# Closing weight sums made by accumulating transfers, inner sums in four slots and later, the decay of two heads later

## The chip, the cores and the metric

The kernel runs on one core of a Trainium2 chip. The metric is device time in microseconds (us). The engines are PE (TensorE: matrix products), DVE (VectorE), ACT (ScalarE), POOL (GpSimd, here mostly an issuer of transfers) and SP (SyncE, which issues most loads). A wait on an engine holds everything queued behind it on that engine.

## The reference

One layer, T = 1024 rows, width 1024, all in float32:

```
h = rms_norm(x, norm_w) * (1 + scale) + shift        # scale, shift, gate = silu(c) @ ada_w + ada_b
hq, hf, hi, hz, gq, gk, gv, gz, ga, mg = split(h @ w_in)
y_h = hgrn2(hq, hf, hi, hz)     # 8 heads, gated linear attention, decay f = lb + (1 - lb) sigmoid(hf)
y_g = gla(gq, gk, gv, gz, ga)   # 4 heads, decay alpha = sigmoid(ga @ alpha_w + alpha_b) ** (1/16)
merged = sigmoid(mg0) * (y_h @ w_branch[0]) + sigmoid(mg1) * (y_g @ w_branch[1])
out = rms_norm(x + gate * (merged @ w_out), final_norm_w)
```

Both attentions run over chunks of 64 rows with a state of 128 keys per head.

## The kernel before, in words

**Number format.** A float32 operand is split in two parts of a shorter format, hi and lo. One product takes three matmuls (hi·hi, hi·lo, lo·hi). L211 (ACT, a cast) makes hi, L212 (DVE, a subtraction) makes lo; L202 and L203 do the same in other places.

**Seven products instead of eight.** Larger products are done as 2x2 blocks by a scheme with seven products in the order 1, 2, 5, 3, 6, 7, 4. Products 5, 6, 3 and 7 (`SUMS`) use sums of weight blocks. These sums are made ahead of time and kept in DRAM: `v_sums` makes them for the inner stages (DRAM tiles `vs`), `prepare` for the closing stages (DRAM tiles `ws`).

**Memory.** 46 slots of SBUF of 4 KB in each partition are lent out by a pool `S`. A slot that was sent to DRAM (`sent=True`) comes free four units later.

**Stages.** A unit is six matmuls of 128x512 of a main product. The main work runs in this order: q and k of the GLA branch; the GLA values (`Vstage`, units 0 to 56); features of GLA (56 to 104); the HGRN values (second `Vstage`, 104 to 160); features of HGRN (`Fstage`, 160 to 216); the remaining features (L607, 216 to 376); the closing stages `last_stages` in four quarters b = 0 to 3 (L1422, 376 to 600); the output product. L2002 is the matmul of the three inner stages. L1860, L1862, L1884 and L1888 take finished sums from PSUM.

**Side work.** `Stream.weave` is called after each unit and advances three tracks, each a queue of generators: `side` (attention heads), `more` and `back`. An entry `[generator, wait, pace, from]` starts at the unit `from`; a generator yields how many units it wants to rest. Heads 0 to 3 are GLA heads, beginning at about units 49, 88, 127 and 166; eight HGRN heads follow every 24 units from 210. A head loads q (and k) on SP (L1054), prepares decayed copies on DVE and ACT (L657 to L771), has its scores on PE (L665 to L767), brings them to SBUF on ACT (L776, L779, L792, L795), and runs the states (L815, L821) and the outputs (L834, L836). L1019 and L1024 close its output.

**The side work that the change touches.**
- `alpha_side((2, 3))`: decay of heads 2 and 3. Four matmuls L389, then ACT L943, DVE L949 and L950, ACT L953 and L956 (Exp, Ln), DVE L957, ACT L960 (Exp). [...]
- `v_sums(s)`: per half four blocks are loaded by SP (L1829), DVE makes four sums (L1832 to L1838, 128x1024 each), POOL stores them (L1840).
- `prepare`: 16 blocks, each two loads of 512 KB by SP (L1258), four additions 128x512 on DVE (L1266 to L1272) and four stores of 256 KB by POOL (L1274). A flag pauses it between the start of the second inner stage and the thirteenth product of the third.
- `gate_side`: loads and a sum for the output gate.

**What sets the order.** The program is written in the order that `weave` gives; a scheduler then orders each engine's queue. Instructions under `held` keep their program order. `Stream.ahead` loads and splits the operands of the next products when enough slots are free.

Of the kernel before, what the change touches and what calls it, by code (L numbers as in the profile page):

```python
# [10 lines left out]
F32 = mybir.dt.float32  # L11
# [3 lines left out]
ALU = mybir.AluOpType  # L15

P = 128
D = 1024
T = 1024
# [13 lines left out]
SUMS = {5: 0, 6: 1, 3: 2, 7: 3}  # L33
# [56 lines left out]
def hybrid_trunk_kernel(  # L90
# [6 lines left out]
    nc = tc.nc  # L97
    x2, o2 = x[0], out[0]
# [4 lines left out]
    dp = ctx.enter_context(tc.tile_pool(name="dram", bufs=1, space=bass.MemoryType.DRAM))  # L103
# [3 lines left out]
    S = Slots(sp, N_SLOTS)  # L107
# [790 lines left out]
    stream = Stream()  # L898
# [353 lines left out]
    paused = [False]  # L1252

    def load_blocks(b, i):
        src = sources[b][i]
        x = [S.get([4, 2, P]) for _ in range(2)]
        for kh in range(2):
            nc.sync.dma_start(x[kh].rearrange("p k a f -> p k (a f)"),  # L1258
                              src[kh * 512:(kh + 1) * 512, :].rearrange("(k p) f -> p k f", p=P))
        return x  # L1260

    def weight_sums(b, i, x1, x2):
        s1, s2 = S.get([2, 4, P]), S.get([2, 4, P])
        parts = {5: s1[:, 0], 6: s1[:, 1], 3: s2[:, 0], 7: s2[:, 1]}
        add = nc.vector.tensor_add
        held(add(parts[7], x1[:, :, 0], x1[:, :, 1]))  # L1266
        yield 1
        held(add(parts[5], x1[:, :, 1], x2[:, :, 1]))
        yield 1
        held(add(parts[6], parts[7], x2[:, :, 1]))  # L1270
        yield 1
        held(add(parts[3], parts[6], x2[:, :, 0]))  # L1272
        for p, q in SUMS.items():
            nc.gpsimd.dma_start(w_sums[b][i // 2][q][:, i % 2 * 512:i % 2 * 512 + 512],  # L1274
                                parts[p].rearrange("p k f -> p (k f)"))
        S.free(x1, x2)
        S.free(s1, s2, sent=True)
        summed_up.add((b, i))

    def prepare():  # L1280
        todo = [(b, i) for b in range(4) for i in range(4)]
        blocks_of = {}
        for n in range(len(todo) + 1):
            while n < len(todo) and (len(S.free_list) < 11 or paused[0]):
                yield 1
            if n < len(todo):
                blocks_of[n] = load_blocks(*todo[n])
            if n:
                yield from weight_sums(*todo[n - 1], *blocks_of.pop(n - 1))
            yield 5  # L1290


    H = {}
# [54 lines left out]
    def load_duo(b, p, j):  # L1348

        t = raw_w[b, p, j] = S.get([2, 512])  # L1350
        if p in SUMS:
            assert {(b, 2 * j), (b, 2 * j + 1)} <= summed_up
            nc.sync.dma_start(t.rearrange("p a f -> p (a f)"), w_sums[b][j][SUMS[p]])
# [465 lines left out]
    def v_sums(s):  # L1819

        add = nc.vector.tensor_add
        for kk in range(2):
            while len(S.free_list) < 9:
                yield 1
            y = {}
            for at_ in ((0, 1), (1, 1), (0, 0), (1, 0)):
                y[at_] = S.get([2, 512])
                for cols, x in w_block(s, *at_, kk):
                    nc.sync.dma_start(y[at_][:, :, cols], x)  # L1829
# [9 lines left out]
            for p, t in ((5, e), (7, y[0, 0]), (6, y[0, 1]), (3, y[1, 0])):  # L1839
                nc.gpsimd.dma_start(vs_d[s][p][kk], t.rearrange("p a f -> p (a f)"))  # L1840
            S.free(y[1, 1])
            S.free(e, y[0, 0], y[0, 1], y[1, 0], sent=True)
            summed_v.add((s, kk))
            yield 2

# [175 lines left out]
    vjobs[0][10].begins = lambda: load_qk(0)  # L2021
    vjobs[0][12].begins = first_head

    def pause(on):
        paused[0] = on

    vjobs[1][0].begins = lambda: pause(True)
    vjobs[2][12].begins = lambda: pause(False)

    def heads_ready(f):  # L2030
        for h in range(2 * f, 2 * f + 2):
# [15 lines left out]
    def front():  # L2047
# [59 lines left out]
```

## Time and profile before

| | us |
|---|---|
| median of three runs (lowest, highest) | 1184.71 (1183.03, 1186.02) |
| the profiled execution | 1183.32 |
| its span | 1181.6 |
| PE busy | 1148.5 |
| DVE busy | 842.1 |
| ACT busy | 648.5 |
| POOL busy | 138.1 |
| mean granted PE clock (1 is full) | 0.994 |

How to read the rows. A timeline row is: start, duration, engine, line, operation, output <- inputs, partitions x elements, count, and in brackets the idle time before it and what released it. A row that ends in "us in total, times, longest" is a wait. In rows by stretch of time (`from:to`), the engines' busy times are followed by the granted PE clock, the share of the 16 DMA engines that was busy, and GB/s. A row of a group of instructions gives busy time and mean ns of one, then idle time before them.

### The profile page before, as it was taken

The page shows a single profiled execution, that of the slowest core. Times are in us where ns is not written, and L with a number is a line of the kernel's source. Part 1 is how long each engine was busy: PE and PEld are TensorE (multiplying, and loading weights), DVE is VectorE, ACT ScalarE, POOL GpSimd, SP SyncE. Part 2 cuts the span into 40 slices and gives each one's busy share as a digit, 9 for nine tenths or more (in the row PEclk, how much of TensorE's full clock was granted, in tenths as well). Part 3 has the DMA queues.
Part 4 walks back from the last instruction along what each step waited for, and adds up shares of the span by engine and source line. Part 5 has one row for each costly group of instructions (what it writes and reads, how often), then busy time and mean ns, then how long its engine had stood idle before and what let it go on. Part 6 is the DMA issues. An engine that isn't in the chain of part 4 may idle for free.

```text
span 1181.6 us, 20555 instructions
## 1 busy us (share of the span) xinstructions
PE 1148.5 (97%) x8089; PEld 942.3 (80%) x8089; DVE 842.1 (71%) x1316; ACT 648.5 (55%) x964; POOL 138.1 (12%) x285
## 2 busy tenths in 40 slices
PE   6999999899999999999999999999999999999997
PEld 5777877688888888788888887878888888888886
DVE  4755669657686636987787688695643866988994
ACT  5675455543664758646455445576643644534654
POOL 5121112010011101222211111001110000000000
PEclk8999999999999999999999999999999999999999
DMA  9847369667476546988865674355798846334523
GB/s 319 279 150 245 143 220 306 204 200 259 143 248 197 186 160 188 293 269 276 255 220 178 222 241 137 100 179 173 258 317 288 284 144 225 119 117 161 181 93 137
DMA packets 155986, 245.56 MB, mean 208 GB/s; under 512 B 10139, under 2 KB 107473, under 8 KB 155890
## 3 DMA queue, kind: packets, MB, share of 16 engines
q1 hardware_dynamic: 134866, 174.10, 46.7%
q0 software_dynamic: 20976, 70.15, 15.6%
q8 instruction: 63, 1.03, 0.3%
q14 instruction: 33, 0.27, 0.1%
q10 hardware_dynamic: 48, 0.01, 0.0%
HBM read 170.29 MB, written 73.92 MB: 207 GB/s over the span
## 4 chain that ended last, share of the span: by engine, by line
PE 62%; issue 22%; DVE 5%; POOL 4%; ACT 4%; DMA 2%; SPq 0%; POOLq 0%; ACTq 0%; DVEq 0%
PE pd L1422 14%; PE pd L2002 12%; PE pd L607 9%; PE sc_ps L1422 6%; PE pm L1422 6%; PE pd L1599 3%; PE sc_ps L1599 2%; PE pm L834 2%; POOL ws L1274 2%; PE pm L836 1%; PE pm L1599 1%; PE pm L815 1%; PE pd L396 1%; DMA b<-in_x_dram 1%; POOL v L1867 1%
## 5 line engine op out<-in xcount | busy, mean ns | idle before, releaser
L607 PE MATMUL pd<-b,b 128*128 128x512 f32 x1248 | 301.6, 396 | 0.0
L607 PEld LDWEIGHTS pd<-b,b 128*128 128x128 f32 x1248 | 230.6, 188 | 48.5
L2002 PE MATMUL pd<-b,b 128*128 128x512 f32 x1008 | 237.8, 393 | 4.2 <-DVE b L1888 2.5
L2002 PEld LDWEIGHTS pd<-b,b 128*128 128x128 f32 x1008 | 187.6, 188 | 45.7 <-ACT b L211 2.9
L1422 PE MATMUL pd<-b,b 128*128 128x512 f32 x720 | 169.4, 390 | 0.0
L1422 PEld LDWEIGHTS pd<-b,b 128*128 128x128 f32 x720 | 134.8, 188 | 28.2
L212 DVE TENSOR_TENSOR b<-b,b 128x1024 fp32r<-128x1024 f32 x92 | 110.9, 1222 | 57.1 <-ACT b L211 52.3
L1365 DVE TENSOR_TENSOR b<-b,b 128x1024 fp32r<-128x1024 f32 x56 | 68.2, 1222 | 57.8 <-ACT b L1364 44.7
L211 ACT CAST b<-b 128x1024 fp32r<-128x1024 f32 x92 | 93.3, 1047 | 11.5 <-PE pd L2002 3.8
L1364 ACT CAST b<-b 128x1024 fp32r<-128x1024 f32 x56 | 58.7, 1051 | 63.3 <-PE pm L1422 17.7
L1422 PE MATMUL sc_ps<-b,b 128*128 128x512 f32 x324 | 77.5, 390 | 0.1
L1342 DVE TENSOR_TENSOR b<-b,b 128x1024 fp32r<-128x1024 f32 x48 | 57.9, 1221 | 23.9 <-ACT b L1341 18.7
L1341 ACT CAST b<-b 128x1024 fp32r<-128x1024 f32 x48 | 49.9, 1051 | 41.5 <-PE pd L1422 16.0
L1422 PE MATMUL pm<-b,b 128*128 128x512 f32 x300 | 71.1, 389 | 0.0
L1422 PEld LDWEIGHTS sc_ps<-b,b 128*128 128x128 f32 x324 | 60.6, 188 | 13.0 <-ACT scT L779 0.5
L1422 PEld LDWEIGHTS pm<-b,b 128*128 128x128 f32 x300 | 56.3, 188 | 11.7
L203 DVE TENSOR_TENSOR b<-b,b 128x1024 fp32r<-128x1024 f32 (+1 forms) x37 | 35.7, 976 | 27.5 <-ACT b L202 27.2
L396 PE MATMUL pd<-b,b 128*128 128x512 f32 x192 | 51.9, 403 | 0.9 <-ACT b L202 0.8
L1274 POOL DMA_DIRECT2D ws<-b x64 | 34.5, 540 | 138.2 <-DVE b L1266 52.8
L834 PE MATMUL pm<-scT,b 128*128 128x128 f32 x256 | 47.5, 278 | 2.8 <-DVE b L821 2.6
L726 DVE TENSOR_TENSOR b<-b,tot 128x512 f32<-128x512 f32 x36 | 24.8, 688 | 30.4 <-PE sc_ps L767 29.2
L834 PEld LDWEIGHTS pm<-scT,b 128*128 128x128 f32 x256 | 38.5, 191 | 7.1 <-DVE b L821 4.8
(333 smaller groups left out, 1749.9 us busy)
## 6 DMA issues: line engine op xcount, KB each, us to landing
b<-in_w_in_dram SPq DMA_DIRECT2D x64, 512.0 KB, 6.0
ws<-b POOLq DMA_DIRECT2D x64, 256.0 KB, 5.4
b<-ws SPq DMA_DIRECT2D x32, 512.0 KB, 4.1
b<-in_w_in_dram SPq DMA_DIRECT2D x52, 256.0 KB, 4.0
b<-fx SPq DMA_DIRECT2D x24, 512.0 KB, 4.7
b<-in_x_dram SPq DMA_DIRECT2D x16, 512.0 KB, 6.1
b<-in_ada_w_dram SPq DMA_DIRECT2D x32, 256.0 KB, 6.4
v<-b POOLq DMA_DIRECT2D x32, 256.0 KB, 4.0
```

The lines of the kernel that those rows point to most:

```text
L211: held(nc.scalar.copy(hi, src))
L212: nc.vector.tensor_sub(lo, src, hi.bitcast(F32))
L396: nc.tensor.matmul(accs[f], wg(a, d, f), b[d][:, half * 512:half * 512 + 512], start=(d == 0 and n == 0), stop=(d == KT - 1 and n == 2))
L607: nc.tensor.matmul(ps[th][0:w, :], a[:, k, 0:w], b[:, th * 512:(th + 1) * 512], start=(k == 0 and n == 0), stop=(k == KT - 1 and n == 2))
L834: nc.tensor.matmul(o, vch(ch)[:, vh * P:(vh + 1) * P], scT[:, ch, :], start=True, stop=(ch == 0))
L1274: nc.gpsimd.dma_start(w_sums[b][i // 2][q][:, i % 2 * 512:i % 2 * 512 + 512], parts[p].rearrange("p k f -> p (k f)"))
L1342: nc.vector.tensor_sub(lo, src, hi.bitcast(F32))
L1364: nc.scalar.copy(hi, t)
L1365: nc.vector.tensor_sub(lo, t, hi.bitcast(F32))
L1422: nc.tensor.matmul(o, a[:, sl], c, start=(p in (1, 5) and kt == 0 and n == 0), stop=(kt == 3 and n == 2), skip_group_check=True)
L1599: nc.tensor.matmul(o, a, b, start=(p in (1, 5) and kt == 0 and n == 0), stop=(kt == 3 and n == 2), skip_group_check=True)
L2002: nc.tensor.matmul(st.bank[i], l_[:, i * P:(i + 1) * P], r_, start=(p in (1, 5) and kk == 0 and a == 0 and n == 0), stop=(kk == 1 and a == ...
```

## The change

Four things are edited.

1. `prepare` makes no sums on DVE any more. For each quarter b it issues 26 transfers on POOL, all from DRAM to DRAM, in the order of a list `CHAIN`: the first block of a sum is copied into `ws`, further blocks are added by the transfer itself (`accum_op=ALU.add`), and two sums start as a copy of another one (1 MB each). A block transfer is 256 KB in rows of 128 floats. There is one unit between two of them and 2.25 more behind each entry of the list. It starts at unit 214, without the pause.
2. `v_sums` adds in place and needs four slots instead of five, in another order of loads and sums; it waits for 8 free slots instead of 9. Both calls start at unit 56, on the track `more`.
3. `alpha_side((2, 3))` goes from `more` (from unit 50) to `back` (from unit 86).
4. `gate_side` starts at unit 300 instead of 320.

```diff
-    w_sums = [[[dp.tile([P, T], F32, name=f"ws{b}{j}{i}") for i in range(4)] for j in range(2)] for b in range(4)]
+    w_sums = [{p: dp.tile([P, 4, 512], F32, name=f"ws{b}{p}") for p in SUMS} for b in range(4)]
...
-    def weight_sums(b, i, x1, x2):
-        s1, s2 = S.get([2, 4, P]), S.get([2, 4, P])
-        parts = {5: s1[:, 0], 6: s1[:, 1], 3: s2[:, 0], 7: s2[:, 1]}
-        add = nc.vector.tensor_add
-        held(add(parts[7], x1[:, :, 0], x1[:, :, 1]))
-        yield 1
-        held(add(parts[5], x1[:, :, 1], x2[:, :, 1]))
-        yield 1
-        held(add(parts[6], parts[7], x2[:, :, 1]))
-        yield 1
-        held(add(parts[3], parts[6], x2[:, :, 0]))
...
+    CHAIN = ((7, (0, 0)), (5, (0, 1)), (7, (0, 1)), (5, (1, 1)), (6, 7), (6, (1, 1)), (3, 6), (3, (1, 0)))
 
     def prepare():
-        todo = [(b, i) for b in range(4) for i in range(4)]
...
+        for b in range(4):
+            def block(kh, a, b=b):
+                src = sources[b]
+                return [src[i][kh * 512:kh * 512 + 512, a * P:a * P + P] for i in range(4)]
+            done = set()
+            for p, src in CHAIN:
+                first = p not in done
+                done.add(p)
+                if isinstance(src, int):
+                    held(nc.gpsimd.dma_start(w_sums[b][p], w_sums[b][src]))
+                else:
+                    for i, x in enumerate(block(*src)):
+                        x = x.rearrange("(k p) f -> p k f", p=P)
+                        y = w_sums[b][p][:, i].rearrange("p (k f) -> p k f", f=P)
+                        if first:
+                            held(nc.gpsimd.dma_start(y, x))
+                        else:
+                            held(nc.gpsimd.dma_start(y, x, accum_op=ALU.add))
+                        yield 1
+                yield 2.25
+            summed_up.add(b)
...
         for kk in range(2):
-            while len(S.free_list) < 9:
+            while len(S.free_list) < 8:
                 yield 1
             y = {}
-            for at_ in ((0, 1), (1, 1), (0, 0), (1, 0)):
+            for at_ in ((0, 1), (0, 0), (1, 1), (1, 0)):
...
-            e = S.get([2, 512])
-            held(add(e, y[0, 1], y[1, 1]))
-            yield 2
             held(add(y[0, 0], y[0, 0], y[0, 1]))
             yield 2
-            held(add(y[0, 1], y[0, 0], y[1, 1]))
+            held(add(y[0, 1], y[0, 1], y[1, 1]))
             yield 2
-            held(nc.vector.scalar_tensor_tensor(y[1, 0], y[0, 1], -1.0, y[1, 0], ALU.mult, ALU.subtract))
...
+            held(add(y[1, 1], y[0, 0], y[1, 1]))
+            yield 2
+            held(nc.vector.scalar_tensor_tensor(y[1, 0], y[1, 1], -1.0, y[1, 0], ALU.mult, ALU.subtract))
...
-        stream.back.append([v_sums(1), 2, 1, 0])
-        stream.back.append([v_sums(2), 2, 1, 0])
-        stream.back.append([prepare(), 4, 1, 0])
-        stream.more.append([alpha_side((2, 3)), 2, 1, 50])
-        stream.more.append([gate_side(), 4, 1, 320])
+        stream.more.append([v_sums(1), 1, 1, 56])
+        stream.more.append([v_sums(2), 1, 1, 56])
+        stream.more.append([gate_side(), 4, 1, 300])
+        stream.back.append([alpha_side((2, 3)), 1, 1, 86])
+        stream.back.append([prepare(), 1, 1, 214])
```

**How the order moves, first place: SP at head 0's loads.** L1054 loads head 0's k and q (DRAM tiles `qk`), L1829 (now L1814) loads blocks for `v_sums`, L589 loads weights of features. Before:

```order
L1054 DMA b_1570<-qk_697 128x1024
L1829 DMA b_1578<-in_w_in_dram 128x2x512
L1054 DMA b_1568<-qk_693 128x1024
L1829 DMA b_1580<-in_w_in_dram 128x2x512
L1829 DMA b_1582<-in_w_in_dram 128x2x512
```

In the changed kernel:

```order
L1054 DMA b_1554<-qk_697 128x1024
L1054 DMA b_1552<-qk_693 128x1024
L589 DMA b_1588<-in_w_in_dram 128x8x128
L589 DMA b_1630<-in_w_in_dram 128x8x128
L589 DMA b_1715<-in_w_in_dram 128x8x128
L1814 DMA b_1813<-in_w_in_dram 128x2x512
```

The `v_sums` loads moved from between and behind head 0's two loads to four rows behind them.

**Second place: DVE at head 0's last decayed copies** (L726, L727, then the mask L771; head 0 reads them on PE at L791). Before:

```order
L726 TENSOR_TENSOR b_1570<-b_1570,tot_772 128x16x32
L727 TENSOR_TENSOR b_1568<-b_1568,tot_772 128x16x32
L729 TENSOR_TENSOR tot_772<-tot_772 128x16
L950 SCALAR_TENSOR_TENSOR b_1762<-b_1871,b_1762 128x1024
L729 TENSOR_TENSOR tot_772<-tot_772 128x8
L957 TENSOR_TENSOR b_1794<-b_1794,b_1735 128x1024
L957 TENSOR_TENSOR b_1871<-b_1871,b_1762 128x1024
L726 TENSOR_TENSOR b_1570<-b_1570,tot_772 128x8x64
L727 TENSOR_TENSOR b_1568<-b_1568,tot_772 128x8x64
L771 COPY_PREDICATED blk<-mask_764,sc_ps_73 128x8x16
```

In the changed kernel:

```order
L727 TENSOR_TENSOR b_1552<-b_1552,tot_772 128x16x32
L742 COPY_PREDICATED blk<-mask_747,sc_ps_72 128x16x4
L726 TENSOR_TENSOR b_1554<-b_1554,tot_772 128x16x32
L726 TENSOR_TENSOR b_1554<-b_1554,tot_772 128x8x64
L727 TENSOR_TENSOR b_1552<-b_1552,tot_772 128x8x64
L771 COPY_PREDICATED blk<-mask_764,sc_ps_73 128x8x16
L1816 TENSOR_TENSOR b_1811<-b_1811,b_1809 128x1024
```

The decay of heads 2 and 3 (L949 to L957) is gone from this place; `v_sums` (L1816) follows behind the mask.

**Third place: DVE and PE ahead of the first summed product (5) of the second inner stage.** This product reads, on PE, b_2797/b_2798 and b_2801/b_2802 before, and b_2832/b_2833 and b_2836/b_2837 in the changed kernel (hi and lo of its two operands). L658 to L669 begin head 2. DVE before:

```order
L212 TENSOR_TENSOR b_2798<-b_2652,b_2797 128x1024
L212 TENSOR_TENSOR b_2802<-b_2654,b_2801 128x1024
L658 TENSOR_TENSOR xb<-b_2853,b_1794 128x32x8
L1024 SCALAR_TENSOR_TENSOR b_2317<-pm_2805,vec,b_2317 128x512
L659 TENSOR_TENSOR xb<-b_2853,b_1794 128x32x8x2
L667 TENSOR_TENSOR b_2853<-b_2853,b_1794 128x256
```

DVE in the changed kernel:

```order
L1024 SCALAR_TENSOR_TENSOR b_2269<-pm_2781,vec,b_2269 128x512
L1818 TENSOR_TENSOR b_2635<-b_2635,b_2641 128x1024
L1030 TENSOR_TENSOR b_2735<-b_2735,b_2778 128x1024
L1820 TENSOR_TENSOR b_2641<-b_2638,b_2641 128x1024
L658 TENSOR_TENSOR xb<-b_2820,b_2350 128x32x8
L659 TENSOR_TENSOR xb<-b_2820,b_2350 128x32x8x2
L667 TENSOR_TENSOR b_2820<-b_2820,b_2350 128x256
L660 TENSOR_TENSOR xb<-xb,b_2350 128x32x16
L661 TENSOR_TENSOR xb<-xb,b_2350 128x32x8
L669 TENSOR_TENSOR b_2350<-b_2350 128x256
L212 TENSOR_TENSOR b_2833<-b_2617,b_2832 128x1024
L212 TENSOR_TENSOR b_2837<-b_2619,b_2836 128x1024
```

PE in the changed kernel:

```order
L1985 MATMUL pd_1_2624<-b_2716,b_155 128x512
L665 MATMUL sc_ps_72<-xb,b_2450 32x80 x16
L665 MATMUL sc_ps_73<-xb,b_2450 32x80
L1985 MATMUL pd_0_2621<-b_2832,b_2836 128x512
L1985 MATMUL pd_1_2622<-b_2832,b_2836 128x512
L1985 MATMUL pd_0_2623<-b_2832,b_2836 128x512
L1985 MATMUL pd_0_2621<-b_2833,b_2836 128x512
```

The two L212 moved from ahead of head 2's start to behind it, with sums of `v_sums(2)` (L1818, L1820) ahead of both; on PE 17 of head 2's score matmuls L665 moved ahead of the product.

More of the change, by code (lines that the diff above doesn't have):

```diff
@@ L1247, in hybrid_trunk_kernel @@
     sources += [[branch(n, d) for d in range(0, 8, 2)] for n in (1, 0)]
-    w_sums = [[[dp.tile([P, T], F32, name=f"ws{b}{j}{i}") for i in range(4)] for j in range(2)] for b in range(4)]
+    w_sums = [{p: dp.tile([P, 4, 512], F32, name=f"ws{b}{p}") for p in SUMS} for b in range(4)]
     summed_up = set()
[L1252 to L1260, printed above, removed]
@@ L1280, in prepare @@
-    def prepare():
-        todo = [(b, i) for b in range(4) for i in range(4)]
[L1282 to L1290, printed above, removed]
+    CHAIN = ((7, (0, 0)), (5, (0, 1)), (7, (0, 1)), (5, (1, 1)), (6, 7), (6, (1, 1)), (3, 6), (3, (1, 0)))
@@ L1351, in load_duo @@
         if p in SUMS:
-            assert {(b, 2 * j), (b, 2 * j + 1)} <= summed_up
-            nc.sync.dma_start(t.rearrange("p a f -> p (a f)"), w_sums[b][j][SUMS[p]])
+            assert b in summed_up
+            nc.sync.dma_start(t, w_sums[b][p][:, 2 * j:2 * j + 2])
         else:
@@ L1830, in v_sums @@
             yield 8
-            e = S.get([2, 512])
-            held(add(e, y[0, 1], y[1, 1]))
-            yield 2
             held(add(y[0, 0], y[0, 0], y[0, 1]))
             yield 2
-            held(add(y[0, 1], y[0, 0], y[1, 1]))
+            held(add(y[0, 1], y[0, 1], y[1, 1]))
             yield 2
-            held(nc.vector.scalar_tensor_tensor(y[1, 0], y[0, 1], -1.0, y[1, 0], ALU.mult, ALU.subtract))
[L1839 to L1842, printed above, removed]
+            held(add(y[1, 1], y[0, 0], y[1, 1]))
+            yield 2
+            held(nc.vector.scalar_tensor_tensor(y[1, 0], y[1, 1], -1.0, y[1, 0], ALU.mult, ALU.subtract))
+            for p, at_ in ((5, (0, 1)), (7, (0, 0)), (6, (1, 1)), (3, (1, 0))):
+                nc.gpsimd.dma_start(vs_d[s][p][kk], y[at_].rearrange("p a f -> p (a f)"))
+            S.free(*y.values(), sent=True)
             summed_v.add((s, kk))
```

10 lines of the change are left out of this document (removed).

## The prediction

> **What bounds the kernel now.** I read the page's busy table first, then the list of PE's waits, then the timelines around the largest of them.
>
> ```profile
> PE 1148.5 (97%) x8089; PEld 942.3 (80%) x8089; DVE 842.1 (71%) x1316; ACT 648.5 (55%) x964; POOL 138.1 (12%) x285
> ```
>
> PE (TensorE) is busy for 1148.5 of 1181.6 us. The change removes none of its matmuls, so it can only win what lies in the other 33 us, or what PE loses while busy at a lower clock. It takes work from DVE (71%), which pays only where a wait on DVE ends last. The first rows of PE's waits (us in all, times, longest):
>
> ```profile
> PE pm L815 <- ACT b L792: 6.1, 6, 3.3
> PE pm L423 <- DVE b L225: 5.4, 3, 4.0
> PE pm L834 <- DVE b L821: 2.6, 6, 0.6
> ```
>
> L423 is the head of the kernel, which the change leaves alone. L815 and L834 are in the attention heads. On PE's timeline the longest wait of L815 stands close behind three others:
>
> ```profile
> 178.36 4.34 PE L2002 MATMUL pd<-b,b 128*128 128x512 f32 x18 [2.55 <-DVE b L1888]
> ...
> 203.71 0.69 PE L767 MATMUL sc_ps<-b,b 128*64 128x64 f32 x16 [0.76 <-DVE b L727]
> ...
> 210.35 0.98 PE L791 MATMUL pm<-ident,b 128*128 128x128 f32 x7 [1.66 <-DVE b L726]
> ...
> 217.34 3.07 PE L815 MATMUL pm<-b,b 128*128 128x256 f32 x8 [3.25 <-ACT b L792]
> 219.84 5.25 PE L607 MATMUL pd<-b,b 128*128 128x512 f32 x18
> ```
>
> All four belong to head 0, the first GLA head: 2.55 + 0.76 + 1.66 + 3.25 = 8.22 us. After the last one the granted clock falls (column PEclk, the number ahead of the DMA share):
>
> ```profile
> 217.00:219.00 2.00, 1.67 (x6) 1.41 (x7) 0.26 (x1) 1.97 (x6) 0.00 (x0) 0.77 0.00 0
> 219.00:221.00 2.00, 2.00 (x6) 1.60 (x5) 1.16 (x4) 0.16 (x1) 0.00 (x0) 0.50 0.00 0
> 221.00:223.00 2.00, 2.00 (x9) 1.58 (x8) 1.97 (x3) 0.00 (x0) 0.13 (x1) 0.87 0.00 0
> ```
>
> The same 8 and 18 matmuls one head later, at full clock:
>
> ```profile
> 288.08 1.89 PE L815 MATMUL pm<-b,b 128*128 128x256 f32 x8
> 289.62 4.44 PE L2002 MATMUL pd<-b,b 128*128 128x512 f32 x18
> ```
>
> From 217.34 to 225.09 is 7.75 us, from 288.08 to 294.06 is 5.98: 1.77 us lost to the clock. The cluster costs 8.22 + 1.77 = 10.0 us.
>
> **Part 1, head 0 without its neighbours (a gain).** Why head 0 is late is seen on DVE and ACT, between 203 and 217 us:
>
> ```profile
> 203.65 1.22 DVE L950 SCALAR_TENSOR_TENSOR b<-b,b 128x1024 f32<-128x1024 f32 x1
> ...
> 204.87 1.22 DVE L957 TENSOR_TENSOR b<-b,b 128x1024 f32<-128x1024 f32 x1
> 208.46 1.23 DVE L957 TENSOR_TENSOR b<-b,b 128x1024 f32<-128x1024 f32 x1 [2.38 <-ACT b L956]
> 209.61 0.69 DVE L726 TENSOR_TENSOR b<-b,tot 128x512 f32<-128x512 f32 x1
> ```
>
> ```profile
> 209.39 1.28 ACT L960 ACT_TABLE_LOAD   x1
> 210.69 2.01 ACT L960 ACTIVATE b<-b 128x1024 f32<-128x1024 f32 x2
> ...
> 216.69 0.98 ACT L792 COPY b<-pm 128x512 f32<-128x512 f32 x2
> ```
>
> L949 to L960 are the decay of heads 2 and 3 (`alpha_side`). DVE waited 2.38 us for its L956 with head 0's L726 queued behind, and ACT ran a table load and both L960 (3.3 us) before the copies L779 and L792 that head 0 needed. In the new order neither DVE nor ACT holds an instruction of `alpha_side` there. What must vanish for PE not to wait at L791 and L815: at L791 1.66 us, against 2.38 of idle plus 3.6 of L950 and L957 on DVE; at L815 3.25, against 3.3 of L960 and what DVE no longer delays. Both fit, so I count 0.76 + 1.66 + 3.25 + 1.77 = 7.4 us as gone. What is late next in that chain is L815 itself, at a few tenths (as in the heads that wait 0.2 to 0.6 each, 2.6 us in 6 at L834).
>
> The 2.55 us at 178 is a load. SP, then the two instructions that waited:
>
> ```profile
> 164.43 0.32 SPq L1054 DMA_DIRECT2D b<-qk  x1
> 164.96 1.95 SPq L1829 DMA_DIRECT2D b<-in_w_in_dram  x3
> ```
>
> ```profile
> 173.22 1.05 ACT L657 COPY xb<-b 128x1024 f32<-128x1024 f32 x1 [5.30 <-DMA b<-qk]
> ```
>
> q of head 0 was issued just ahead of three 512-KB loads of `v_sums` (and in SP's order behind a fourth). ACT idled 5.30 us, the casts L211 and L212 for the next product came late, and L1888 behind them. Now head 0's two loads stand one behind the other, and the `v_sums` loads come four rows later. I count the 2.55 as gone.
>
> **Part 2, the first summed product of the second stage (a loss).** `v_sums(2)` and the prefetch for this product now meet head 2's start. PE's next product cannot start before 17 of head 2's L665, which read what DVE's L661 leaves, and needs the two L212 behind it. Durations from before, where DVE did the two L212 first:
>
> ```profile
> 308.80 0.65 DVE L658 TENSOR_TENSOR xb<-b,b 128x256 f32<-128x256 f32 x1 [2.03 <-DMA b<-qk]
> 309.37 0.74 DVE L1024 SCALAR_TENSOR_TENSOR b<-pm,vec,b 128x512 f32<-128x512 f32 x1
> 310.03 0.86 DVE L659 TENSOR_TENSOR xb<-b,b 128x512 f32<-128x512 f32 x1
> 310.76 0.63 DVE L667 TENSOR_TENSOR b<-b,b 128x256 f32<-128x256 f32 x1
> ...
> 313.06 0.91 DVE L660 TENSOR_TENSOR xb<-xb,b 128x512 f32<-128x512 f32 x1
> 314.00 0.67 DVE L661 TENSOR_TENSOR xb<-xb,b 128x256 f32<-128x256 f32 x1
> ...
> 318.30 2.36 DVE L212 TENSOR_TENSOR b<-b,b 128x1024 fp32r<-128x1024 f32 x2
> ```
>
> ```profile
> 319.27 11.05 PE L2002 MATMUL pd<-b,b 128*128 128x512 f32 x48
> ```
>
> One matmul is 11.05/48 = 0.23 us. Let zero be the moment when PE ends the product before the previous one; the previous one is 24 matmuls, 5.4 us. On DVE: L1024 to 0.3 (its PE work ends 1.4 us ahead of zero, six matmuls, and ACT's L1019 lies between), two additions of `v_sums` and L1030 (1.22 us each like L950, one every 1.15 as they overlap) to 3.8, then L658, L659, L667, L660, L661 (their rows: 3.7, overlapping by 0.1 each: 3.3) to 7.1, L669 0.55, two L212 at 1.15 to 9.9. PE waits at L665 from 5.4 to 7.1, and reaches the first matmul that needs the second L212 (17 short L665 and eight matmuls later, without waits at 5.4 + 0.35 + 1.8 = 7.6) at 9.9 or 10: a new stall of about 2.4 us. That holds if head 2's q has landed by 3.8. Its load is issued at about zero, since its slot is read by the previous product's last matmul:
>
> ```profile
> DMA to landing us min/median/max: 3.1/4.4/6.7
> ```
>
> That is the answer on L1054, all six such loads. At 3.1 us the stall is 2.4, at 4.4 it is 3.0, at 6.7 it is 5.3; I take 3.0. The other end is nothing: with DVE 2.4 us earlier than reckoned by hand, there is no stall.
>
> Whether the clock falls after it: the 2.55 us at 178 cost none, the 3.25 at 217, which came 7 us behind another 1.66, cost 1.77. 3.0 lies between and stands alone; I put down 0.5.
>
> The Trainium skill, "TensorE: Matmul & The Clock Gate", Part 1, says that the clock halves after an idle window of about 3.4 us. The trace does not quite agree: 3.25 us sufficed. By that rule a stall of 3.0 costs no clock and the sum would be 0.5 lower; by the row of 3.25 it would be 1.3 higher.
>
> **Part 3, sums by accumulating transfers (near nothing, unsure).** DVE loses 64 additions in four groups like this one, 44 us in all, between 470 and 790 us:
>
> ```profile
> L1268 DVE TENSOR_TENSOR b<-b,b 128x512 f32<-128x512 f32 x16 | 11.0, 689 | 0.0
> ```
>
> PE's waits there are most of the 2.6 us at L834 and of the 6.1 - 3.3 = 2.8 at L815, tenths each. SP loses 32 loads of 512 KB, POOL 64 puts. POOL gains 104 transfers, DRAM to DRAM: 96 of 256 KB in rows of 512 bytes, 64 of them adding, and 8 copies of 1 MB. What an issue costs:
>
> ```profile
> L1274 POOL DMA_DIRECT2D ws<-b x64 | 34.5, 540 | 138.2 <-DVE b L1266 52.8 <-DVE b L1272 41.4 <-DVE b L1268 24.8
> ```
>
> 104 at 0.54 is 56 us of an engine that is 12% busy, against 34.5 before: hidden. A lighter DVE may give back some 2 us of those waits. What the transfers cost no row shows, because no transfer before adds or goes from DRAM to DRAM. Bounds by neighbours:
>
> ```profile
> q1 hardware_dynamic: 134866, 174.10, 46.7%
> q0 software_dynamic: 20976, 70.15, 15.6%
> ```
>
> q1's mean packet (1291 bytes) takes 0.467 x 1181.6 x 16 / 134866 = 0.065 us of an engine; q0's 3344 bytes take 0.141, or 0.022 per 512 bytes. The 49,152 packets then take 66 to 200 us of all sixteen engines, where the removed 33.6 MB took about 97 (53 on q1, 44 on q0, by the same rates). So the load lies between 10 lower (with 22 for the copies) and 125 higher over some 320 us, at a share that was (tenths by slices of 29.5 us, the 17th to the 27th here, 0.63 to 0.73 in the mean):
>
> ```profile
> DMA  9847369667476546988865674355798846334523
> ```
>
> I take +0.5 us in all, from -2 (small waits gone) to +3 (loads late). The sums of a quarter are ready long before they are read, so their own latency counts for nothing.
>
> **The sum.** -10.0 + 3.0 + 0.5 + 0.5 = -6.0 us. Against the profiled execution's 1183.32 that gives 1177.3; the median of the three runs is 1184.71, 1.4 above it, so I forecast 1178.7.
>
> **Rivals.**
>
> *The new stall does not come.* DVE's order puts head 2 ahead of the next product, but my hand schedule has no row to lean on, and 2.4 us is six short instructions. Then -10.0 + 0.5 = -9.5: 1175.2. For it: DVE idles there before (the 2.03 at 308.80). Against it: it now has three 1.2-us additions to do. Chance 0.2.
>
> *The stalls only move.* `alpha_side` now starts beside head 1, with its table loads and `v_sums`. If it does to head 1 what it did to head 0, 7.4 us come back: -6.0 + 7.4 = +1.4, or 1186.1. Against it: reckoned by hand with the durations above, ACT has 1.5 to 2 us to spare at head 1's copies, an estimate. Chance 0.17.
>
> *The adding transfers crowd the others out.* Slower. Place: 470 to 790 us, eight HGRN heads. If an adding packet is paid twice (its destination is read too), 81,920 packets at 0.065 take 335 us of sixteen engines in 320; without the removed part the rest took 0.68 x 320 - 97 = 121, and 22 for the copies, so it decides from (320 - 143) x 16 / 49,152 = 0.058 us per mean packet. Loads then land as at 160 to 175 us, where q of head 0 waited behind others and cost 2.55 us. Six such waits are 15.3: -6.0 + 15.3 = +9.3, or 1194. Against it: loads have their own queue and the slots are roomy. Chance 0.13.
>
> Half the bytes take two thirds of the time on SP's queue:
>
> ```profile
> b<-in_w_in_dram SPq DMA_DIRECT2D x64, 512.0 KB, 6.0
> ...
> b<-in_w_in_dram SPq DMA_DIRECT2D x52, 256.0 KB, 4.0
> ```
>
> The Trainium skill, "DMA: Bandwidth & Descriptors", Rules for kernel authors, speaks against the change here: it asks for 1 MiB or more per transfer, and says that an accumulating one reads its destination and writes it later. With the first the two rows agree in kind; the second no run here shows yet.
>
> **How the numbers follow.** My forecast has 0.5, the rivals 0.2, 0.17 and 0.13. 0.3% is 3.6 us, about what a measurement can tell: faster is below 1181.1, slower above 1188.3. The forecast's own spread (stall 2.4 to 5.3, clock 0 to 1.8, transfers -2 to +3) is 1175.6 to 1184; about 0.43 of its 0.5 lies below 1181.1. With the first rival: faster 0.63, same 0.22 (the rest, and the stalls that move), slower 0.15. The range goes from 1173 to 1188: it holds the first rival and the moved stalls, and leaves out the last.
>
> **What would show it.** Right: no wait above 1 us at L791 and L815 of head 0, no stall at its first L665; a new wait of 2 to 5 us at head 2's L665 just ahead of the second stage's first summed product (some 10 us earlier than 317); full clock after both; the same pace from 470 to 790. Wrong: waits of 1 to 3 us at head 1's L791 or L815; in the list of transfers, loads of 512 KB that land in 8 us or more; PE waits on slots or loads after 470.

## The result and the profile after

The changed kernel is slower: 1197.56 us median (1196.93 to 1198.4, 4 runs), against 1185.13 beside it (1183.03 to 1186.02). The ratio is 1.0109, 95% interval 1.0094 to 1.0124. The prediction said 1178.7, with a range from 1173 to 1188.

Where the time went is seen by comparing when PE starts the same matmul of 128x512 in both traces. Numbered from 0, in us (after less before):

```
matmul no.              780     1160    1780    2040    last
it starts before at     226.0   335.7   519.4   597.0   1174.8
changed kernel          -10.2   -3.2    +8.3    +14.2   +13.6
```

So there are three parts: 10.2 us won at head 0, 7.0 lost between 226 and 336 us, 16.8 lost behind that, nearly all before 600 us. In finer steps, with the times of the kernel before, 11.6 us of the last part fall between 487 and 525 us and 6.8 between 562 and 597; 1.4 come back between 707 and 746. Single traces can't be read more finely than some 3 us: the kernels below that have the same program up to the closing sums stand between -1.7 and -4.8 at matmul 1160, and between -1.2 and +1.5 already at the first matmul, which no edit touches.

The page's busy row and queue rows, to be held against those of before:

```profile
PE 1154.8 (97%) x8089; PEld 947.3 (79%) x8089; DVE 807.2 (68%) x1252; ACT 646.1 (54%) x963; POOL 215.9 (18%) x325
...
q1 hardware_dynamic: 117970, 157.32, 41.6%
q0 software_dynamic: 52464, 86.93, 27.9%
```

DVE lost 35 us of work and POOL gained 78 us: 104 issues cost POOL not 0.54 us each but 2 us and more where they add. PE's waits after:

```profile
PE sc_ps L756 <- ACT xb L718: 8.6, 1, 8.6
PE sc_ps L698 <- DVE xb L694: 5.5, 2, 5.0
...
PE pm L834 <- DVE b L821: 2.7, 4, 0.9
PE pd L1985 <- ACT b L211: 2.4, 1, 2.4
...
PE sc_ps L665 <- DVE xb L661: 2.3, 2, 1.4
```

Head 0's four waits (L1888, L767, L791, L792) are gone. In their place stand the two at L756 and L698, which are the starts of HGRN heads, and two at L1985 and L665. On PE's timeline of the changed kernel:

```profile
308.84 0.85 PE L665 MATMUL sc_ps<-xb,b 128*32 128x80 f32 x34 [1.39 <-DVE xb L661]
...
324.49 0.80 PE L1985 MATMUL pd<-b,b 128*128 128x512 f32 x1 [2.40 <-ACT b L211]
...
501.15 0.74 PE L756 MATMUL sc_ps<-xb 128*16 128x16 f32 x64 [8.57 <-ACT xb L718]
503.13 0.66 PE L762 MATMUL sc_ps<-xb 128*32 128x32 f32 x32 [1.25 <-ACT xb L718]
...
585.37 1.51 PE L698 MATMUL sc_ps<-xb,b 128*32 128x48 f32 x64 [5.04 <-DVE xb L694]
```

What released the longest of them is read backwards: PE waited for ACT's L718, and ACT in turn stood before an activation of the next head (L1147, which reads f), queued ahead of three of the four L718:

```profile
499.53 1.06 ACT L1147 ACTIVATE b<-b 128x1024 f32<-128x1024 f32 x1 [9.91 <-DMA b<-f]
500.50 1.12 ACT L718 COPY xb<-b 128x512 f32<-128x512 f32 x2
```

In the kernel before, ACT ran all four L718 first and came to the same L1147 much later:

```profile
495.90 0.62 ACT L718 COPY xb<-b 128x512 f32<-128x512 f32 x1 [0.17 <-DVE b L726]
504.71 1.28 ACT L1147 ACT_TABLE_LOAD   x1
```

The second long wait (5.04 us at 585) begins at a load of f too, but POOL's queue comes ahead of it. POOL waited 8.31 us for landings of its own chain, with two stores of yg queued behind, which could have gone some 2 us sooner (DVE's L981 ended at 556.1). They landed after 6.7 and 7.2 us; SP held the load of f 5.5 us for them; ACT waited 7.69 us for the load. DVE's L694 then stood behind L1200, L981 and L1149, which waited for ACT (12.50, 1.75 and 1.15 us).

```profile
557.93 0.54 POOL L1264 DMA_DIRECT2D ws<-ws  x1 [8.31 <-DMA ws<-in_w_in_dram]
558.45 1.14 POOL L906 DMA_DIRECT2D yg<-b  x2
```

```profile
572.36 1.28 ACT L1147 ACT_TABLE_LOAD   x1 [7.69 <-DMA b<-f]
```

The load of f behind the first wait, on SP, and what POOL issued at the same time:

```profile
480.49 1.44 SPq L589 DMA_DIRECT2D b<-in_w_in_dram  x2
484.39 3.63 SPq L1143 DMA_DIRECT2D b<-f  x1
```

```profile
479.72 0.77 POOL L1270 DMA_DIRECT2D ws<-in_w_in_dram  x1
480.51 0.54 POOL L1892 DMA_DIRECT2D f<-b  x1
481.05 5.30 POOL L1270 DMA_DIRECT2D ws<-in_w_in_dram  x7
486.74 1.30 POOL L1272 DMA_DIRECT2D ws<-in_w_in_dram  x1 [0.40 <-DMA f<-b]
489.13 3.81 POOL L1272 DMA_DIRECT2D ws<-in_w_in_dram  x3 [1.09 <-DMA ws<-in_w_in_dram]
```

SP began to issue the load at 484.4 and ACT went on at 499.5: 15 us, where the two such loads at this place took 9.7 and 10.1 before (7.6 is the median of all eight). The issue alone lasted 3.63 us here, 0.72 at most there; what held it, the trace does not settle. Twelve transfers of `ws` (L1270 copies, L1272 adds) were issued in 13 us. The program spaces them by a unit each, but that sets only their place in POOL's queue: the first eight have nothing to wait for, and so they come at POOL's own pace. The DMA engines from 480 to 500 us:

```profile
q0 software_dynamic: 2699, 3.79, 81.9%
q1 hardware_dynamic: 2224, 1.57, 29.2%
...
ws<-in_w_in_dram POOLq DMA_DIRECT2D x12, 256.0 KB, 9.1
b<-in_w_in_dram SPq DMA_DIRECT2D x2, 512.0 KB, 13.8
```

q0 (POOL's) holds 82% of the engines' time, q1 (SP's) 29% (they overlap a little), and SP's loads of 512 KB land after 13.8 us. And, as after head 0 before, PE's granted clock falls behind the wait:

```profile
490.00:496.00 6.00, 2.58 (x12) 1.80 (x10) 0.80 (x6) 0.00 (x0) 2.94 (x3) 0.93 1.17 271
496.00:502.00 6.00, 0.74 (x64) 0.63 (x64) 0.87 (x2) 2.47 (x4) 0.00 (x0) 0.50 1.10 166
502.00:504.00 2.00, 0.86 (x33) 0.80 (x34) 1.81 (x4) 2.00 (x3) 0.00 (x0) 0.50 0.03 4
```

So two things meet at the first wait: f lands late, and ACT's queue needs it sooner (ACT was ready for it at 489.6 us). In the old order a load that ends at 499.5 us would have been in time (ACT comes to L1147 at 504.7 us before, and at 500.8 in experiment 1). That is read from these rows; no run below has ACT's old order with the transfers at full size.

The theory from here on: **crowding**. The transfers of `ws` fill the DMA engines just when the next HGRN head loads q and f. The rival: **order**. Without the old loads and additions SP puts two weight loads (L589) ahead of f, the moved decay and inner sums shift everything, and the transfers' bytes are innocent. A second question within crowding: is it the adding, the short rows, the bytes, or the burst?

### The profile page after: what moved, and what is told of

Read it like the earlier page. It is cut to its first block, busy times and chain, and to the rows that moved or that the text cites. A ratio compares the mean times of both kernels' runs of the same rounds, so it can differ in the third digit from the quotient of the medians.

```text
span 1195.2 us, 20372 instructions
## 1 busy us (share of the span) xinstructions
PE 1154.8 (97%) x8089; PEld 947.3 (79%) x8089; DVE 807.2 (68%) x1252; ACT 646.1 (54%) x963; POOL 215.9 (18%) x325
## 3 DMA queue, kind: packets, MB, share of 16 engines
q1 hardware_dynamic: 117970, 157.32, 41.6%
q0 software_dynamic: 52464, 86.93, 27.9%
## 4 chain that ended last, share of the span: by engine, by line
PE 77%; DVE 8%; ACT 6%; DMA 5%; issue 2%; SPq 1%; POOL 0%; ACTq 0%; DVEq 0%; POOLq 0%
PE pd L1985 16%; PE pd L607 15%; PE pd L1407 14%; PE sc_ps L1407 6%; PE pm L1407 6%; PE pd L396 3%; PE pd L1584 3%; PE pm L834 2%; PE sc_ps L1584 2%; DMA b<-f 2%; PE pm L836 2%; PE pm L815 1%; PE sc_ps L396 1%; PE pm L1584 1%; DMA b<-in_ada_w_dram 1%
## 5 line engine op out<-in xcount | busy, mean ns | idle before, releaser
L1985 PE MATMUL pd<-b,b 128*128 128x512 f32 x1008 | 239.7, 395 | 3.8 <-ACT b L211 2.4
L1985 PEld LDWEIGHTS pd<-b,b 128*128 128x128 f32 x1008 | 188.0, 188 | 46.4 <-ACT b L211 2.8
L212 DVE TENSOR_TENSOR b<-b,b 128x1024 fp32r<-128x1024 f32 x92 | 110.7, 1221 | 53.5 <-ACT b L211 52.0
L211 ACT CAST b<-b 128x1024 fp32r<-128x1024 f32 x92 | 93.6, 1048 | 14.2 <-DMA v<-b 5.0
L726 DVE TENSOR_TENSOR b<-b,tot 128x512 f32<-128x512 f32 x36 | 24.7, 687 | 42.4 <-PE sc_ps L767 30.1
L1272 POOL DMA_DIRECT2D ws<-in_w_branch_dram x32 | 41.7, 2191 | 30.7 <-DMA ws<-ws 30.5
L1272 POOL DMA_DIRECT2D ws<-in_w_in_dram x32 | 41.3, 2273 | 18.4 <-DMA ws<-ws 16.9
```

The source lines that it names most:

```text
L211: held(nc.scalar.copy(hi, src))
L212: nc.vector.tensor_sub(lo, src, hi.bitcast(F32))
L1272: held(nc.gpsimd.dma_start(y, x, accum_op=ALU.add))
L1985: nc.tensor.matmul(st.bank[i], l_[:, i * P:(i + 1) * P], r_, start=(p in (1, 5) and kk == 0 and a == 0 and n == 0), stop=(kk == 1 and a == ...
```

## The experiments

Diffs are against the changed kernel unless it is said otherwise. Where it is of use, four numbers follow a result: how much later (+) or earlier (-) than before, in us, PE starts matmul 1160, 1780, 2040 and the last. The changed kernel has -3.2, +8.3, +14.2, +13.6. The kernel before was measured again beside each group of runs; its medians lie between 1182.87 and 1185.13 us, and each ratio is to the one beside it.

**1. The old closing sums, everything else changed.**

```diff
-        stream.back.append([prepare(), 1, 1, 214])      # transfers from DRAM to DRAM
+        stream.back.append([prepare(), 4, 1, 208])      # load_blocks, weight_sums of the kernel before
```

> The changed kernel, but with the old closing sums (SP loads, DVE additions, POOL stores, from unit 208), so only the inner sums, the decay and the gate are moved. Crowding theory (the adding transfers fill the DMA engines and HGRN heads get q and f late): all that was lost behind 450 us comes back, and what is left is the 10.2 us won at head 0 less the 7 lost between 300 and 333 us: about 1182, and no wait above 1 us behind 450. Order theory (the moved decay and inner sums shift SP's and DVE's order so that heads load late, the transfers are innocent): the waits at L756 and L698 behind 480 us stay, 1192 to 1198.

1176.99 us (ratio 0.9941, 0.9926 to 0.9956): -3.5, -3.8, -4.5, -6.4. No wait above 1 us behind 450 us:

```profile
PE pd L2000 <- ACT b L211: 2.4, 1, 2.4
PE sc_ps L665 <- DVE xb L661: 2.3, 2, 1.4
PE pm L815 <- ACT b L792: 1.9, 6, 0.5
PE pm L834 <- DVE b L821: 1.9, 3, 0.7
```

It is 5 us better than expected: 1.6 of that because the kernel before stood at 1183.56 beside it and not at 1185.13, and some 3 by small waits between 500 and 740 us that also went. The new closing sums cost 20.6 us (1197.56 less 1176.99), or 19.0 with each held against the kernel before beside it.

**2. The new closing sums alone, on the kernel before.** (`prepare`, `CHAIN` and the load of `ws` as in the changed kernel; the pause goes. Against before:)

```diff
-        stream.back.append([prepare(), 4, 1, 0])        # load_blocks, weight_sums
+        stream.back.append([prepare(), 1, 1, 214])      # CHAIN, transfers from DRAM to DRAM
...
-    vjobs[1][0].begins = lambda: pause(True)
-    vjobs[2][12].begins = lambda: pause(False)
```

> The kernel before, with nothing but the new closing sums. Crowding theory: the stalls of head 0 stay, none comes at 300 to 333 us, and behind 450 us about 16 us are lost as in the changed kernel (from 3.2 ahead to 13.6 behind): 1197 to 1203. Order theory: 1185, within 3 us.

1207.6 us (ratio 1.0211, 1.0183 to 1.0238): -0.1, +11.0, +17.7, +23.4. The transfers alone lose 23 us, more than the crowding theory's 1197 to 1203; 17.7 of them by 600 us, much as in the changed kernel, and some 6 more at 816 us, where a head waits for ACT, and ACT for a store (4.32 us <-DMA yh<-b). The order theory's 1185 is out: the moved decay and inner sums are not needed for the loss. The old loads and additions are missing here too, and ACT's L1147 (table load at 491.49 us) again stands ahead of three L718, so that half of the order theory is not touched.

**3. Plain copies instead of additions.** (The sums are left out: each addition overwrites.)

```diff
-                            held(nc.gpsimd.dma_start(y, x, accum_op=ALU.add))
+                            held(nc.gpsimd.dma_start(y, x))
```

> The changed kernel with every adding transfer made a plain copy to the same place: as many transfers, rows and bytes, but no sums, so the closing stages multiply by other weights. If reading the destination and adding is what costs: POOL's issue falls from 2.25 us to about 0.75 each, the transfers land in 5 us or less instead of 9, most of the 16 us behind 450 us come back: 1181 to 1187. If copies from DRAM to DRAM in rows of 512 bytes cost it whether they add or not: 1194 to 1199 and landings of 8 us or more.

1193.94 us (ratio 1.0087, 1.0072 to 1.0102): -3.5, +8.4, +11.2, +10.3. Only 3.6 us came back (2.0 with each held against the kernel before beside it, and the intervals of the two ratios overlap), though the transfers themselves became much cheaper:

```profile
q0 software_dynamic: 23792, 86.93, 20.6%
```

```profile
L1272 POOL DMA_DIRECT2D ws<-in_w_in_dram x32 | 23.7, 746 | 21.7 <-DMA ws<-ws 17.4 <-DMA ws<-in_w_in_dram 3.3 <-DMA yh<-b 0.4
```

An issue costs 0.75 us instead of 2.25 in the median, and 28,672 packets vanish, 448 for each of the 64 transfers. But the first burst, eight plain copies and four more, is as before, and so is the wait of 8.6 us at L756; the one at L698 is 2.75 instead of 5.04, and POOL comes to the two stores of yg at 556.4 us instead of 558.4. So the adding is at most a small part.

**4. The decay alone, later, on the kernel before.** (Diff against before.)

```diff
-        stream.more.append([alpha_side((2, 3)), 2, 1, 50])
+        stream.more.append([alpha_side((2, 3)), 2, 1, 86])
```

> The kernel before with one number changed: the decay of heads 2 and 3 starts at unit 86 instead of 50. If the decay was what made head 0 late, 7 to 7.5 us of the 10.2 go (waits at L767, L791, L815 and the half clock), the 2.5 us of the q load stay: 1177 to 1179. If the inner sums beside head 0 were as much to blame, or head 1 now waits instead: 1182 to 1186.

1182.27 us (ratio 0.9987, 0.9977 to 0.9996). Head 0 is mended as expected (-6.8 at matmul 780), but 5.3 us of it come back at once (-1.5 at 1160), at head 1:

```profile
272.35 0.69 PE L756 MATMUL sc_ps<-xb 128*16 128x16 f32 x64 [0.50 <-ACT xb L718]
274.51 0.64 PE L762 MATMUL sc_ps<-xb 128*32 128x32 f32 x32 [1.47 <-DVE blk L742]
275.62 1.12 PE L767 MATMUL sc_ps<-b,b 128*64 128x64 f32 x16 [0.46 <-DVE b L727]
```

```profile
266.45 1.28 ACT L956 ACT_TABLE_LOAD   x1
267.74 1.15 ACT L956 ACTIVATE b<-b,ones 128x1024 f32<-128x1024 f32 x1
268.91 1.28 ACT L960 ACT_TABLE_LOAD   x1
270.21 1.06 ACT L960 ACTIVATE b<-b 128x1024 f32<-128x1024 f32 x1
271.17 1.12 ACT L718 COPY xb<-b 128x512 f32<-128x512 f32 x2
```

The table loads and activations of the decay stand ahead of L718, now those of head 1, and the clock is at 0.57 from 274 to 282 us. The stalls moved, as the second rival of the prediction had it; in the changed kernel they did not (PE waited 0.45 us at head 1's L815). There the inner sums lie otherwise and the decay is on another track; no run tells which of the two it was.

**5. As 1, and the second inner sums from unit 118.**

```diff
-        stream.more.append([v_sums(2), 1, 1, 56])
+        stream.more.append([v_sums(2), 1, 1, 118])
```

> The changed kernel with the old closing sums (as in the first experiment, 1177.0) and the second call of the inner sums starting at unit 118 instead of 56. DVE's order ahead of the first summed product of the second stage is then again the one of before (both L212 ahead of head 2's L658). Theory that the new stalls at 308 and 324 us come from the inner sums beside head 2's start: both go, with their half clock, some 5 to 7 us: 1170 to 1172. Rival, that the later inner sums hold up heads 2 or 3 instead: 1176 to 1180.

1173.05 us (ratio 0.9907, 0.989 to 0.9923): -8.5, -7.5, -8.4, -10.0. The stalls at 308 and 324 us are replaced by one of 1.5 and two of 0.5; 3.9 us of the 7 come back, so the result lies between the two ranges expected. This kernel beats both.

**6. Transfers of a quarter of the bytes.** (The sums are left out; the closing stages load other data of the same size.)

```diff
-                        x = x.rearrange("(k p) f -> p k f", p=P)
+                        x = x.rearrange("(k p) f -> p k f", p=P)[:, 0:1]
...
-            nc.sync.dma_start(t, w_sums[b][p][:, 2 * j:2 * j + 2])
+            nc.sync.dma_start(t.rearrange("p a f -> p (a f)"), f_x[p][j])
```

> The changed kernel with all 104 transfers kept in number, place and waits, but each of a quarter of the bytes, and the closing stages load other data of the same size instead of the sums (so the sums are left out). The order of every engine is that of the changed kernel. Crowding theory: the loads of f land in time, the waits at L756 and L698 go, most of the 16.8 us lost between 333 us and the end come back: 1180 to 1185. Order theory (without the old loads and additions SP puts two weight loads ahead of the f load, and POOL's queue waits on itself; the bytes are innocent): 1194 to 1198, waits at L756 of over 5 us.

1178.77 us (ratio 0.9958, 0.9943 to 0.9973): -4.7, -4.2, -5.1, -6.2. With the same order on PE, DVE and ACT, 18.8 us come back (17.2 with each held against the kernel before beside it), the wait at L756 is gone and none at L698 is above 0.7 us. So order alone is not to blame: the bytes are needed, whether they slow the loads or make POOL wait longer for its chain. That the order has no part is not shown, since this kernel too has ACT's new order. From 480 to 500 us:

```profile
q1 hardware_dynamic: 3699, 2.32, 37.4%
q0 software_dynamic: 945, 1.12, 27.2%
...
b<-in_w_in_dram SPq DMA_DIRECT2D x2, 512.0 KB, 7.8
ws<-in_w_in_dram POOLq DMA_DIRECT2D x11, 64.0 KB, 5.0
```

The two weight loads land after 7.8 us instead of 13.8.

**7. Rows of 1 KB instead of 512 bytes.** (Other weights are summed.)

```diff
-                return [src[i][kh * 512:kh * 512 + 512, a * P:a * P + P] for i in range(4)]
+                return [src[i][kh * 512 + a * 256:kh * 512 + a * 256 + 256, :] for i in range(4)]
```

> The changed kernel with the source of each 256-KB transfer taken as 256 rows of 1 KB instead of 512 rows of 512 bytes: the same bytes and transfers, other weights are summed. If the short rows are what makes the transfers dear: landings fall from 9 us to 6 or less, half of the loss or more comes back, 1184 to 1190. If it is DRAM to DRAM as such, or the burst: 1194 to 1198.

1196.81 us (ratio 1.0116, 1.0098 to 1.0134), landings 8.9 and 9.7 us, and 11.3 us of wait at L756: the rows are not it.

**8. Two units between block transfers.**

```diff
                            held(nc.gpsimd.dma_start(y, x, accum_op=ALU.add))
-                        yield 1
+                        yield 2
```

> The changed kernel with two units instead of one between block transfers, so that the same 104 transfers are spread over about twice the time. Crowding theory: fewer of them stand beside any one load, the waits at L756 and L698 shrink to 2 us or less each: 1184 to 1190. Order theory: 1194 to 1198, the waits only move.

1229.38 us (ratio 1.0382, 1.0367 to 1.0398). -2.8, +4.7, +12.5, +46.6: a miss for both theories. The rest between them hardly spreads the burst. POOL still issued the eight copies from 480.2 to 488.2 us, with one wait of 1.44 us among them; only the four additions came later, behind a store of yh for which POOL waited 30.61 us, and the wait at L756 is 5.57 us instead of 8.57. The rest also moves later transfers among POOL's other stores and into the closing stages, where 35 us more are lost.

**9. Pairs: the two copies of a column block, then the two additions on them.** (Same transfers and sums, another order, so that POOL has to wait for a landing every two transfers.)

```diff
-            for p, src in CHAIN:
...
+            for i in range(4):
+                put(7, (0, 0), i, True)
+                yield 1
+                put(5, (0, 1), i, True)
+                yield 1
+                put(7, (0, 1), i)
+                yield 1
+                put(5, (1, 1), i)
...
+            for p, q, src in ((6, 7, (1, 1)), (3, 6, (1, 0))):
```

Here `put` issues one transfer, with `True` a plain copy, otherwise an addition.

> The changed kernel with the transfers of each quarter in another order: for each of the four column blocks the two plain copies and the two additions on top of them come one behind the other, so that POOL has to wait for a landing after every two transfers, where the changed kernel issued twelve in 11 us without any wait. Same transfers, rows, bytes and sums. If the burst at 480 to 490 us is what made the load of f late: the wait at L756 falls from 8.6 to below 3 us, and the time to 1185 to 1192. If the bytes cost the same however they are spread: 1195 to 1200.

1198.78 us (ratio 1.0129, 1.0071 to 1.0188): -2.5, 0.0, +0.5, +13.6. At 745 us the kernel stands at -0.8 instead of +13.7: without the burst the wait at L756 is 0.6. Then 13.4 us are lost in one place:

```profile
806.16 1.51 PE L698 MATMUL sc_ps<-xb,b 128*32 128x48 f32 x64 [11.67 <-ACT xb L692]
```

```profile
803.75 1.06 ACT L1331 ACTIVATE b<-b 128x1024 fp32r<-128x1024 f32 x1 [11.39 <-DMA yh<-b]
```

```profile
790.03 0.54 POOL L1277 DMA_DIRECT2D ws<-ws  x1 [13.60 <-DMA ws<-in_w_branch_dram]
796.55 1.25 POOL L1265 DMA_DIRECT2D ws<-in_w_branch_dram  x1 [5.98 <-DMA ws<-ws]
797.31 1.64 POOL L906 DMA_DIRECT2D yh<-b  x2
```

POOL waits 13.6 and then 6 us for the chain's own landings, the stores of yh (L906) stand behind that, and the closing stage's ACT, with the head's L692 queued behind it, waits for yh.

**10. The closing sums from unit 226.**

```diff
-        stream.back.append([prepare(), 1, 1, 214])
+        stream.back.append([prepare(), 1, 1, 226])
```

> The changed kernel with the closing sums starting at unit 226 instead of 214, behind the load of f that landed late. If the burst is what matters, the wait at L756 near 492 us goes and the burst meets a later load instead or none: 1186 to 1194. If it is the bytes over the whole stretch: 1195 to 1200.

1203.41 us (ratio 1.0176, 1.0159 to 1.0193): -1.7, +4.2, +6.8, +19.7. As expected at the first head (a wait of 2.7 us at L756 instead of 8.6), but above both ranges in the sum: a wait of 12.1 us at 839 us came, behind ACT's 14.12 us for a store of `gate`, which stood in POOL's queue behind the chain as in 9.

**11 and 12. Pairs with less rest, from unit 204; and that with the inner sums from unit 118.**

```diff
-        stream.back.append([prepare(), 1, 1, 214])
+        stream.back.append([prepare(), 1, 1, 204])      # and rests of 0.75 and 1 instead of 1 and 2.25
```

> The kernel of the ninth experiment (additions in pairs, 1198.8, where a wait of 11.7 us at 794 us had taken the place of the one at 492) with the closing sums starting at unit 204 and less rest between the transfers, so that the chain ends some 40 units earlier. Theory: the wait at 794 came from POOL, where the stores of yh stood behind the chain's own waits; with the chain over by then it goes, and the time is 1180 to 1186. Rival, that the last quarter's bytes slow the closing stages' loads themselves, or that POOL now holds up the stores of f: 1192 or more.

> The same with the second call of the inner sums from unit 118, which took 3.9 us off with the old closing sums. Expected some 4 us below the run beside it. It is the best that the new closing sums have here, to be held against 1173.0 with the old ones: if adding in the transfers is worth anything, it has to come out below that; by the bytes and POOL's waits I expect 1176 to 1182.

1270.9 us (ratio 1.0736, 1.0699 to 1.0774) and 1267.51 (1.0725, 1.0685 to 1.0764): far off what was expected, but for the 3.4 us between the two (some 4 were expected). The wait at 794 went, but POOL now holds up everything earlier. SP in the eleventh:

```profile
SPq L589 <- DMA yg<-b: 28.7, 1, 28.7
...
SPq L1143 <- DMA yg<-b: 26.4, 1, 26.4
```

SP's loads wait for slots that come free when POOL's stores of yg have landed, and those stand behind additions that wait for their predecessors. PE waits 12.1 us at the first head again, 28.3 at another, 16.5 and 32.8 at two more. So the rival in the expectation, POOL's queue, was right in kind: it named the stores of f, and it is those of yg.

## Why the prediction was wrong

**Part 1 was right in size.** 10.0 us were expected at head 0, and 10.2 came (-10.2 at matmul 780). The 2.55 us of the load of q came too: the changed kernel is 2.6 us ahead at matmul 660. The reason holds for the decay: it alone, moved, gave 6.8 of the expected 7.4 at head 0 (experiment 4). That head 1 would have time enough for the decay held in the changed kernel, but it was a matter of what stands beside it: in experiment 4 it did not.

**Part 2 was right in kind and half in size.** The stall at head 2's L665 came, with 1.39 us; 1.7 of the 2.4 to 3.0 were reckoned there, and the rest at the second L212, where PE did not wait. (The 17 matmuls of L665 in the order are 34 in the trace, 0.85 us and not 0.35.) The step that failed is that it was counted as the only one: one product later PE waited 2.40 us for L211, which stood on ACT behind two table loads and the activations of head 1's L994 and L995 (318.1 to 323.0 us). The clock went to 0.63 and 0.52 behind it, over 2 us each, which is 1.7 us. The two waits and the clock make 5.5 of the 7.0 us lost there, where 3.5 were expected; the other 1.5 are not accounted for. Experiment 5 shows for 3.9 us that the inner sums at that place are the cause.

**Part 3 is the step that decided.** It put the 104 transfers at +0.5 us, -2 to +3, and they cost 19 to 21 (experiment 1) or, with the order kept, 17 to 19 for their bytes (experiment 6). Its own sign of being wrong came: loads of 512 KB landed after 13.8 us. Four things in it were wrong.
- The bound was an average. It had the load of all sixteen engines between 10 us lower and 125 higher, over some 320 us. The real load lies in that bound: q0 takes 27.9% of 1195.2 us against 15.8% of 1175.2 in experiment 1, q1 41.6% against 46.7%, so 96 us more of sixteen engines. But the plain copies of experiment 3 add only some 6 us by the same sum, and still lose 17 us against experiment 1. What counts is which loads they stand beside: twelve transfers in 13 us next to one load of f. With the same bytes and no such burst, the wait there was 0.6 us (experiment 9).
- "Loads have their own queue" was given as an argument against the rival. The queues share the engines: 82% to 29%.
- It looked at DVE's and SP's queues where work was taken out, and not at ACT's. There the activation that reads f came to stand ahead of the copies that PE needed (L1147 before L718), so that a late f stopped PE. How much of the loss would remain in ACT's old order is open.
- POOL was called hidden by its busy share. Its queue is in order: a wait for the landing of one transfer holds the stores of yh, yg and gate behind it. In the changed kernel this is part of the second wait (5.04 us at 585), and it is what killed each attempt to spread or move the burst (8 to 12).

The third rival, 1194 with a chance of 0.13, was near the result, and named the place and the loads. Its reason was another: that an adding packet is paid twice. Shown is that the adding costs 2 to 3.6 us here, at the edge of what the runs can tell, and the transfers as such the rest. That the number was near is luck: it reckoned six waits of 2.55 us, and two of 8.57 and 5.04 came, with the clock behind them and 3.5 us more lost in part 2. The forecast's chance for faster was 0.63.

The Trainium skill, "DMA: Bandwidth & Descriptors", Queues, rings and completion order, says that each DMA engine goes round the queues that it has work for, packet by packet. The shares of 82% and 29% fit that in kind, if POOL's packets are the longer ones in these 20 us (1404 bytes against 706 in the mean); no run here varied the length of SP's own packets, so it stays an inference.

Left open: why PE's small waits for ACT and DVE between 500 and 740 us are 3 us fewer in experiment 1 than before (half of it near 725 us, where PE waited 1.64 us at L815 before; the changed kernel gains as much there), and why the runs of experiment 9 spread by 18 us (1188.39 to 1206.21) where the others agree within 8.

## What to carry to other kernels

Work that is moved from an engine to transfers is not gone: look at which loads are in flight at the moment, not at the mean share of the DMA engines, and at what stands behind the reader of such a load in its engine's queue. Remember too that a rest between issues in the program order does not pace a queue that has nothing to wait for. A queue that issues both a chain of dependent transfers and other work's stores makes every store wait for the chain. And a helper that stalls one head will stall the next if it is only moved there: each place has to be looked at by what else runs beside it.

## What the runs showed of the hardware

- An adding transfer from DRAM to DRAM counts one packet per row, a plain one far fewer: 448 packets less for each of the 64 when they become plain copies (512 to 64 by that), 256 less with rows of 1 KB (52,464 to 36,080 packets).
- Its issue on POOL takes 2.25 us in the median for the blocks of w_in (1.99 for those of w_branch) and 1.24 at least. A plain copy's takes 0.74 when all are plain; among additions it is 0.75 for w_in and 2.05 for w_branch. A store from SBUF takes 0.54.
- Landing of 256 KB: 9.0 to 9.6 us for the mix in the changed kernel, 6.7 to 6.8 when all are plain, beside 2.8 to 5.9 for stores from SBUF (medians).
- The granted clock falls to half behind a wait of PE of 2.4 us too (0.52 from 326 to 328 us, in a stretch with another wait of 1.39 us 15 us earlier), where a wait of 2.55 us before cost nothing.
